# Two chained transformer blocks: experts' rows fetched by indirect DMA, sums kept in x1's place, and weight pieces loaded as two neighbouring rows per partition

## The chip, the cores and the metric

The kernel runs on one core of one Trainium2 chip. The metric is device time in microseconds (us) of one execution; the profiled execution is one of these, recorded by the hardware profiler. All times below are in us unless they are marked ns. [...]

## The reference, cut to what matters

Two blocks follow each other on 512 tokens of width 1024, all in float32. The first has attention and a short convolution, merged and projected, and then a mixture of 16 experts; the second is a chain of dense layers. The change lies around the experts:

```
hx2    = rmsnorm(x1, norm2_g) * (1 + sc2) + sh2          # 512 x 1024
aff    = softmax(hx2 @ w_router)                         # 512 x 16
gate, idx = top_k(aff.T, 64)                             # each expert picks 64 tokens
xe     = hx2[idx]                                        # 16 x 64 x 1024
ye     = (silu(xe @ w_gate) * (xe @ w_up)) @ w_down * gate
x2     = x1 + g2 * scatter_add(ye, idx)
```

Each expert has three matrices of 1024 x 1024 float32, 4 MiB each: 192 MiB of weights for 64 rows per expert.

## The kernel before, in words

The program is one long list of instructions, in the order in which the code emits them. The mixture of experts comes after the first block's output projection (x1, held in SBUF as four tiles `xr` of 128 tokens) and ahead of the second block's dense layers.

**Router.** `half_T` and `half_mm` transpose x1 by pieces of 128 columns, multiply by the router weights `wr_` and fill `aff`; `s1` holds each token's inverse norm (its last step is a power on GpSimd). `router_aff` turns `aff` so that experts lie on partitions. Eight rounds of max and match_replace on VectorE mark each expert's 64 tokens, a scan numbers them, and `post` holds, per token and expert, the slot number or 0.

**Experts, in pairs.** Eight pairs p of experts (two experts share the 128 columns of TensorE, 64 slots each). `onehot(p)` compares slot numbers with 1..64: `Gu` is the 0/1 matrix token x slot, `Gs` the same times `s1`. `gather(p, k0, n)` multiplies x1 by `Gs`, 128 columns at a time, which picks, scales and transposes the tokens' rows in one step; ScalarE applies gain and shift and writes `xe`. Then come three matmuls over the weights (`pair_gemm`: `pa_` for gate, `pu` for up, `py` for down), each in four steps of two pieces (one piece of 1 MiB per expert: 256 rows of a matrix, as two blocks of 128 rows). `hb` is the activated product, transposed on TensorE ahead of the down matmul. `put_y` scales by the gate column `gt_` (made by `gates`), and `combine` adds the pair's rows to the tokens through `GT`, the transposed 0/1 matrix (made by `slots_T`); the sums live in two tiles `acc`. The gather of pair p+1 is laid between the steps of pair p's down matmul.

**Weights.** `elist` is the list of 192 MiB in the order of use: 184 pieces of 256 x 1024 (1 MiB each), and then the last pair's down matrices, 8 MiB, by column halves (512 columns). `eload` takes the next piece of the list, a free tile of the pool that a just consumed piece came from, and issues the load on SyncE's queue (SP). Twenty pieces are loaded ahead of the first matmul; from then on a load is issued when a step of `pair_gemm` has consumed a piece, except for the piece numbers in one line:

```
if i not in (3, 15, 16, 17, 18):
    eload(etiles[i][1])
```

Those five tiles go to `GT`, `hb`, `yb`, `acc` and others. A piece is laid out as `w.rearrange("(k p) n -> p k n", p=128)`: partition p gets row p and row 128 + p of the piece, two runs of 4 KB.

**Around it.** VectorE, ScalarE, GpSimd and SP each work through their own queue in order. `pw_tile` computes a product for the second block between router and experts and writes it to HBM (`pw_d`) from ScalarE's queue; it is read back late in the second block as runs of 8 KB. `x2_half` finishes x2 as the last combine's halves come, and the second block's first weights (`W.load`) stand behind the experts' in SP's queue.

Of the kernel before, what the change touches and what calls it, by code (L numbers as in the profile page):

```python
# [18 lines left out]
NT = T // 128  # L19
# [11 lines left out]

CL = _layout(("ident", 128), ("sel", 2), ("iota", 64),
             ("cos", NT * HD), ("sin", NT * HD), ("mask", 896), ("cmask", 128))


def _constants():

    c = np.zeros((128, CL["total"]), np.float32)
    p = np.arange(128)
    c[:, CL["ident"]] = np.eye(128, dtype=np.float32)  # L40
    for i in range(2):
        c[:, CL["sel"].start + i] = (p % 32 == i)
    t = np.arange(T)
    inv = np.float32(10000.0) ** (-np.arange(16, dtype=np.float32) / np.float32(16))
# [18 lines left out]
def tile_two_blocks(ctx: ExitStack, tc: tile.TileContext, a, out):  # L63
# [311 lines left out]
    ACT.activation(sT[:, :, 0:2], p_[:, :16].rearrange("p (i k) -> p k i", i=2), AF.Silu)  # L375
    modc = cp.tile([128, 48, 2], F32, name="modc")

# [165 lines left out]
    wr_ = cp.tile([128, KT, 16], F32, name="wr_")  # L543
    SP.dma_start(out=wr_, in_=a["w_router"][0].rearrange("(k p) e -> p k e", p=128))
    wk = W.parts[0]
# [208 lines left out]
    def mod_hooks(h, dst, add, after):  # L754
# [16 lines left out]
        return hooks  # L771

    def mod_columns(c, acc_):

        p_ = bank("pb", (4,))
        for j in range(4):
            PE.matmul(p_[:, j:j + 1], acc_[:, j * 128:j * 128 + 128], onec, start=True, stop=True)
        DVE.tensor_add(modc[:, c:c + 4, 0], p_, column("b_mod", c, 4))

# [222 lines left out]
    def half(n):  # L1002
        return slice(n * 512, n * 512 + 512)

    ga2 = cp.tile([128, 8], F32, name="ga2")
    DVE.tensor_scalar(ga2, modc[:, 32:40, 0], 1.0, None, op0=OP.add)
    DVE.tensor_mul(ga2, ga2, column("norm2_g", 0, 8))
    sh2 = modc[:, 24:32, 0]
    rb = cp.tile([128, 16], F32, name="rb")

    def router_prep():
# [36 lines left out]
    def half_mm(t, n):  # L1048
# [31 lines left out]
    def eload(tags):  # L1080

        for tag in tags.split():
            i = len(etiles)
            if i < len(elist) and not (tag == "wr" and i >= len(elist) - 14):
                w, k, nc_ = elist[i]
                if tag == "X":

                    t_ = [gp.tile([128, D], F32, name="ewa", tag="g1b"),
                          cp.tile([128, CL["cmask"].start - nc0], F32, name="ewb", tag="cst2")[:, 0:D]]
                    for j in range(2):  # L1090
                        SP.dma_start(out=t_[j], in_=w[128 * j:128 * j + 128])
# [98 lines left out]

    Gu, Gs = {}, {}

    def onehot(p):

        Gu[p], Gs[p] = tmp("Gu", (NT, 128)), tmp("Gs", (NT, 128))
# [3 lines left out]
        DVE.tensor_mul(Gs[p], Gu[p], s1[:, :, None].to_broadcast([128, NT, 128]))  # L1199

    onehot(0)
    def gather(p, k0, n=4):

        p_ = bank("pg", (n, 128))
        for d in range(n):
            ds = slice((k0 + d) * 128, (k0 + d) * 128 + 128)
            for t in range(NT):
                PE.matmul(p_[:, d], xrow(t, ds), Gs[p][:, t], start=(t == 0), stop=(t == NT - 1))  # L1208
        for d in range(n):
            k = k0 + d  # L1210
# [110 lines left out]
    for p in range(8):  # L1321
# [23 lines left out]
        side = []
        if p < 7:
            gather(p + 1, 0, 2)
            side = [lambda q=q: gather(p + 1, 2 * q, 2) for q in (1, 2, 3)]
# [533 lines left out]
```

## Time and profile before

| what | value |
|---|---|
| median of 3 runs | 1700.84 us (1697.22 to 1701.57) |
| profiled execution, its own time | 1697.36 us |
| its span, first to last instruction | 1695.6 us |
| mean granted TensorE clock | 0.998 |
| TensorE matmul busy | 1657.6 us (98%) |
| VectorE, ScalarE, GpSimd busy | 917.1, 582.1, 49.5 us |
| HBM read, written | 329.94 MB, 4.19 MB |

The 98% of TensorE is an average over stages with different limits, and matmuls are pipelined, so a busy TensorE can still be one that has to wait for data a little at each step. The page's DMA and GB/s lines cut the span in 40 slices of 42.4 us and show which stage moves how much.

### The profile page before, as it was taken

What the parts mean: (1) busy time and instruction counts of PE and PEld (TensorE: products, weight loads), DVE (VectorE), ACT (ScalarE), POOL (GpSimd) and SP (SyncE); (2) the same over time, 40 slices, a digit from 0 to 9 for tenths busy, and PEclk for the clock granted to TensorE, in tenths of its full rate; (3) what the DMA queues carried; (4) which work ended last, traced back from release to release, by engine and by line L of the source; (5) the groups of instructions that cost most, each with busy time, mean ns of one, the idle gap of its engine ahead of it and who ended that gap; (6) DMA issues with size and microseconds to landing.
All of it is one profiled execution on the core that took longest, in us unless ns stands there. A gap on an engine that the chain in (4) does not pass through costs nothing.

```text
span 1695.6 us, 21458 instructions
## 1 busy us (share of the span) xinstructions
PE 1657.6 (98%) x8704; PEld 1173.6 (69%) x8704; DVE 917.1 (54%) x1687; ACT 582.1 (34%) x1118; POOL 49.5 (3%) x59
## 2 busy tenths in 40 slices
PE   8999999989999999999999999989999999999998
PEld 5987787767888874443444344358898888877886
DVE  4667776565564442212212211257889999845555
ACT  5454444455232232110111011053435442354234
POOL 2000000000000000000000000010001000000000
PEclk9999999999999999999999999999999999999999
DMA  9232323111554669999999999953323233333241
GB/s 337 88 125 75 125 75 100 58 43 52 174 180 142 246 271 344 361 399 409 409 409 409 409 409 408 403 199 109 100 75 100 75 99 97 102 100 100 100 149 50
DMA packets 162167, 335.52 MB, mean 198 GB/s; under 512 B 6959, under 2 KB 91732, under 8 KB 161812
## 3 DMA queue, kind: packets, MB, share of 16 engines
q1 hardware_dynamic: 159376, 328.50, 53.4%
q0 software_dynamic: 1168, 2.89, 0.5%
q10 hardware_dynamic: 1524, 2.76, 0.4%
q8 instruction: 68, 1.11, 0.3%
q14 instruction: 31, 0.25, 0.0%
HBM read 329.94 MB, written 4.19 MB: 197 GB/s over the span
## 4 chain that ended last, share of the span: by engine, by line
PE 90%; DVE 6%; ACT 2%; issue 1%; DMA 1%; POOL 0%; SPq 0%; POOLq 0%; ACTq 0%; DVEq 0%
PE pb L294 15%; PE pb L295 15%; PE pb L296 15%; PE pu L1244 7%; PE py L1244 6%; PE pg L1208 4%; PE po L873 2%; PE pT L865 2%; PE s L834 1%; PE pg L1265 1%; PE pv L295 1%; PE pv L296 1%; PE pv L294 1%; PE pa__5938 L1244 1%; PE pa__7273 L1244 1%
## 5 line engine op out<-in xcount | busy, mean ns | idle before, releaser
L253 DVE TENSOR_TENSOR wl<-wr,wh 128x512 fp32r<-128x512 f32 x340 | 230.1, 696 | 119.6 <-ACT wh L255 119.6
L255 ACT ACTIVATE wh<-wr 128x512 fp32r<-128x512 f32 x340 | 194.6, 620 | 104.8 <-PE pb L295 58.9
L1593 DVE SCALAR_TENSOR_TENSOR co<-cin,cols,co 128x512 f32<-128x512 f32 x240 | 191.5, 798 | 4.2
L294 PE MATMUL pb<-h2h,wh 128*128 128x512 f32 x432 | 170.8, 395 | 0.0
L296 PE MATMUL pb<-h2h,wl 128*128 128x512 f32 x432 | 168.3, 390 | 0.0
L295 PE MATMUL pb<-h2l,wh 128*128 128x512 f32 x432 | 168.2, 389 | 0.0
L294 PE MATMUL pb<-hxh,wh 128*128 128x512 f32 x320 | 130.1, 406 | 0.0
L295 PE MATMUL pb<-hxl,wh 128*128 128x512 f32 x320 | 125.3, 392 | 0.0
L296 PE MATMUL pb<-hxh,wl 128*128 128x512 f32 x320 | 125.3, 391 | 0.0
L1244 PE MATMUL pu<-ew,xe 128*64 128x512 f32 x512 | 116.0, 595 | 0.0
L1244 PE MATMUL py<-ew,hb 128*64 128x512 f32 x440 | 101.0, 597 | 0.0
L294 PEld LDWEIGHTS pb<-h2h,wh 128*128 128x128 f32 x432 | 81.1, 188 | 18.9 <-issue 2.4
L296 PEld LDWEIGHTS pb<-h2h,wl 128*128 128x128 f32 x432 | 81.1, 188 | 17.1
L295 PEld LDWEIGHTS pb<-h2l,wh 128*128 128x128 f32 x432 | 81.2, 188 | 16.9 <-issue 0.5
L1279 DVE SCALAR_TENSOR_TENSOR yt<-py,gt__5666,g2b 128x512 f32<-128x512 f32 x15 | 10.6, 747 | 143.8 <-PE py L1244 136.3
L1244 PEld LDWEIGHTS pu<-ew,xe 128*64 128x64 f32 x512 | 36.4, 137 | 66.4 <-issue 64.6
L844 ACT ACTIVATE P<-P,m 128x512 f32<-128x512 f32 (+1 forms) x64 | 49.7, 777 | 85.6 <-DVE m L843 83.1
L840 DVE CUSTOM_DVE_ANT_0 P<-s,cst,sink 128x512 f32<-128x512 f32 (+1 forms) x64 | 52.2, 816 | 46.0 <-PE s L837 45.7
L1211 ACT ACTIVATE xe<-pg,modc,ga 128x128 f32<-128x128 f32 x64 | 25.8, 453 | 147.0 <-PE pg L1208 140.5
L1208 PEld LDWEIGHTS pg<-Gs,xr 128*128 128x128 f32 x512 | 59.5, 191 | 20.9 <-issue 19.5
L296 PEld LDWEIGHTS pb<-hxh,wl 128*128 128x128 f32 x320 | 60.0, 188 | 13.3
L294 PEld LDWEIGHTS pb<-hxh,wh 128*128 128x128 f32 x320 | 60.2, 188 | 11.4 <-issue 2.3
(453 smaller groups left out, 3066.9 us busy)
## 6 DMA issues: line engine op xcount, KB each, us to landing
ew<-w_exp_gate SPq DMA_DIRECT2D x64, 1024.0 KB, 18.1
ew<-w_exp_up SPq DMA_DIRECT2D x64, 1024.0 KB, 16.7
ew<-w_exp_down SPq DMA_DIRECT2D x59, 1024.0 KB, 15.7
wr<-w_in SPq DMA_DIRECT2D x58, 1024.0 KB, 5.8
wr<-w_mod SPq DMA_DIRECT2D x16, 1024.0 KB, 5.1
wm<-w_mod SPq DMA_DIRECT2D x8, 1024.0 KB, 13.6
wr<-w_out SPq DMA_DIRECT2D x8, 1024.0 KB, 5.0
wr<-w_proj_attn SPq DMA_DIRECT2D x4, 1024.0 KB, 5.2
```

The costliest lines, as they stand in the source:

```text
L253: (lo_engine or DVE).tensor_tensor(lo[:, ks], raw[:, ks], hi[:, ks].bitcast(F32), op=OP.subtract)
L255: ACT.activation(hi[:, ks], raw[:, ks], AF.Copy)
L294: PE.matmul(ps, ah, bh, start=first, stop=False)
L295: PE.matmul(ps, ah, bl, start=False, stop=False)
L296: PE.matmul(ps, al, bh, start=False, stop=last)
L840: DVE.tensor_tensor_reduce(p_[:, :n], s2[:, self.s0:self.s0 + n], self.mask, 1.0, sink8[:, 4 * g + i:4 * g + i + 1], op0=OP.add, op1=OP.ma ...
L844: ACT.activation(p_[:, :n], p_[:, :n], AF.Exp, bias=m4[:, i:i + 1], scale=0.125, accum_out=sm[:, i:i + 1])
L865: PE.transpose(p_[:, i, :], self.P[i][:, kk * 128:kk * 128 + 128], ident)
L873: PE.matmul(po[64 * h:64 * h + 64], V[:, vi, g * 64:g * 64 + 64], last[:, :, h, :], start=(kk == 1), stop=(kk == nk), tile_position=(0, 64 ...
L1208: PE.matmul(p_[:, d], xrow(t, ds), Gs[p][:, t], start=(t == 0), stop=(t == NT - 1))
L1244: PE.matmul(ps[64 * e:64 * e + 64, n], lhs(k, e), tiles[e][kk][:, n * 512:n * 512 + 512], start=(k == 0), stop=(k == KT - 1), tile_positio ...
L1593: DVE.scalar_tensor_tensor(co[ct], cin[ct][:, k:k + 512], ctap(k, ct), co[ct], op0=OP.mult, op1=OP.add)
```

## The change

1. x1's rows are written to HBM (`x1_d`, four stores of 512 KB on ScalarE's queue) as they are finished. For pairs 1 to 7 the rows of the experts come back by an indirect DMA issued by GpSimd (128 rows of 4 KB), whose indices are made on TensorE and VectorE by `gates(p)` from the 0/1 matrix and a column of token numbers; ScalarE scales the rows by the inverse norm, `slots` transposes them on TensorE and VectorE applies gain and shift. Pair 0 is still gathered by matmul.
2. The sums go into x1's own tiles; `acc` is gone, and pieces 16 and 17 are reloaded like the others.
3. A piece is laid out as `(p k) n -> p (k n)`: partition p gets rows 2p and 2p + 1, one run of 8 KB. All that meets this order (x1's columns, `hb`, gain, shift, router weights) is read with a step of two (`dcol`). The last pair's column halves become 16 loads of 512 KB with runs of 2 KB, as before.
4. A `pad` tile and smaller `modc` move the weight tiles by 64 bytes inside a partition.

```diff
+    bmp = cp.tile([128, 32], F32, name="bmp")
+    for i, (n, o) in enumerate((("b_mod", 3072), ("b_mod", 4096), ("norm2_g", 0))):
...
+        POOL.dma_start(out=bmp[:, 8 * i:8 * i + 8].rearrange("p (q k) -> p q k", k=2), in_=v_)
...
+    def dcol(k):
+
+        return slice(256 * (k // 2) + k % 2, 256 * (k // 2) + 256, 2)
...
-            c = n * 512 + i * 128
-            PE.transpose(p_[:, i], xrow(t, slice(c, c + 128)), ident)
+            PE.transpose(p_[:, i], xrow(t, dcol(4 * n + i)), ident)
...
+            DVE.tensor_copy(aff[:, t, 17:18], s1[:, t:t + 1])
+            ACT.dma_start(out=x1_d[t * 128:t * 128 + 128], in_=xrow(t))
...
-                SP.dma_start(out=t_, in_=w.rearrange("(k p) n -> p k n", p=128))
+                for j in range(0, k, 2):
+                    SP.dma_start(out=t_[:, j:j + 2], in_=w[128 * j:128 * j + 256].rearrange("(p k) n -> p k n", k=2))
...
+        if p:
+            r = xe[:, p % 2].rearrange("p k c -> p (k c)")
+            POOL.indirect_dma_start(out=r, out_offset=None, in_=x1_d,
+                                    in_offset=bass.IndirectOffsetOnAxis(ap=ix[:, p:p + 1], axis=0))
+            ACT.activation(r, r, AF.Copy, scale=sl[:, p:p + 1])
+
+    def slots(p, n):
+
+        r = xe[:, p % 2].rearrange("p k c -> p (k c)")
+        p_ = bank("pg", (4, 128))
+        for i in range(4):
+            PE.transpose(p_[:, i], r[:, dcol(4 * n + i)], ident)
+        for i in range(4):
+            k = 4 * n + i
+            DVE.tensor_scalar(xe[:, p % 2, k], p_[:, i], ga2[:, k:k + 1], sh2[:, k:k + 1], op0=OP.mult, op1=OP.add)
...
-                if i not in (3, 15, 16, 17, 18):
+                if i not in (3, 15, 18):
...
-        DVE.tensor_add(arow(t, half(n)), p_, (arow if p else xrow)(t, half(n)))
+        DVE.tensor_add(xrow(t, half(n)), p_, xrow(t, half(n)))
...
-        side = [lambda: None, lambda: None, lambda: gates(p)] + ([lambda: slots_T(p)] if p else [])
+        side = [lambda: gates(p + 1) if p < 7 else None, lambda: gates(0) if not p else None]
...
+        if p < 6:
+            onehot(p + 2)
+        side = []
+        if p < 7:
+            slots(p + 1, 0)
+            side = [lambda: None, lambda: slots(p + 1, 1)]
```

How TensorE's queue changes, from the up matmul of pair 2 to the start of its down matmul (`pu` and `py` are the two sums, `Gs` and `xr` the matmul gather, `Gu` the 0/1 matrix). Before:

```order
L1244 MATMUL pu<-ew,xe 64x512 x16
L1218 MATMUL pg<-aff,Gu 128x2 x4
L1244 MATMUL pu<-ew,xe 64x512 x8
L1230 MATMUL pg<-cst,Gu 128x128 x4
L1244 MATMUL pu<-ew,xe 64x512 x8
L1208 MATMUL pg<-Gs,xr_5042 128x128 x2
L1208 MATMUL pg<-Gs,xr_5043 128x128 x2
L1208 MATMUL pg<-Gs,xr_5042 128x128 x2
L1208 MATMUL pg<-Gs,xr_5043 128x128 x2
L1353 MATMUL pg<-cst,hb 128x128 x8
```

And now, at the same place:

```order
L1243 MATMUL pg<-aff,Gu 128x18 x4
L1287 MATMUL pu<-ew,xe 64x512 x32
L1273 MATMUL pg<-cst,Gu 128x128 x4
L1384 MATMUL pg<-cst,hb 128x128 x8
L1261 MATMUL pg<-cst,xe 128x128 x4
L1287 MATMUL py<-ew,hb 64x512 x8
L1261 MATMUL pg<-cst,xe 128x128 x4
```

The gather's matmuls are gone; `gates` for the next pair stands ahead of the whole up matmul, and eight transposes of the fetched rows stand around the first step of the down matmul.

ScalarE's queue over one pair (`hb` the activation of the gate sums, `GT` the transposed 0/1 matrix, `yb` the pair's output). Before:

```order
L1337 ACTIVATE hb<-pa__6206 128x512 x2
L1231 ACTIVATE GT<-pg 128x512
L1211 ACTIVATE xe<-pg,modc,ga_5046 128x128 x2
L1358 ACTIVATE hb<-pg 128x512
L1211 ACTIVATE xe<-pg,modc,ga_5046 128x128 x6
L1280 ACTIVATE yb<-yt 128x512 x2
```

And now, at the same place:

```order
L1374 ACTIVATE hb<-pa__6187 128x512 x2
L1254 ACTIVATE xe<-xe,sl 128x1024
L1274 ACTIVATE GT<-pg 128x512
L1389 ACTIVATE hb<-pg 128x512
L1317 ACTIVATE yb<-yt 128x512 x2
```

One pass over the fetched rows, which waits for the indirect DMA, has come ahead of `GT` and of the copy of `hb` that the down matmul needs.

## Rows read from the trace of the kernel before

**Rows 1.** The page: GB/s in 40 slices, and all DMA packets by size.
```profile
GB/s 337 88 125 75 125 75 100 58 43 52 174 180 142 246 271 344 361 399 409 409 409 409 409 409 408 403 199 109 100 75 100 75 99 97 102 100 100 100 149 50
DMA packets 162167, 335.52 MB, mean 198 GB/s; under 512 B 6959, under 2 KB 91732, under 8 KB 161812
```

**Rows 2.** Windows of the experts' stage: busy by engine, then clock, DMA share, GB/s.
```profile
668.00:686.00 18.00, 18.00 (x88) 6.48 (x86) 1.69 (x4) 1.08 (x2) 0.00 (x0) 1.00 0.93 365
686.00:700.00 14.00, 13.54 (x82) 7.35 (x79) 1.98 (x3) 2.69 (x6) 0.00 (x0) 1.00 0.90 358
700.00:720.00 20.00, 20.00 (x104) 9.11 (x103) 4.30 (x7) 2.87 (x6) 0.00 (x0) 1.00 0.92 343
720.00:740.00 20.00, 19.69 (x91) 7.42 (x92) 5.32 (x10) 1.08 (x2) 0.00 (x0) 1.00 1.01 388
760.00:1060.00 300.00, 296.12 (x1506) 130.47 (x1506) 57.73 (x95) 33.93 (x72) 0.00 (x0) 1.00 1.03 409
1100.00:1112.00 12.00, 11.44 (x48) 3.46 (x48) 2.60 (x8) 0.63 (x1) 0.00 (x0) 1.00 1.05 386
```

**Rows 3.** Timeline of SP's queue: start, duration, what; pair 1's gate pieces.
```profile
668.80 14.77 SPq L1096 DMA_DIRECT2D ew<-w_exp_gate  x8
```

**Rows 4.** Chain of waits near the stage's end: start, duration, what.
```profile
1098.51 11.78 DMA ew<-w_exp_down
```

**Rows 5.** Timeline of TensorE: pair 2's and 3's first steps; last expert matmuls.
```profile
769.15 3.60 PE L1244 MATMUL pa__6206<-ew,xe 128*64 128x512 f32 x16
...
827.58 2.74 PE L1244 MATMUL pa__6472<-ew,xe 128*64 128x512 f32 x12
...
1116.31 1.94 PE L1400 MATMUL py<-ew,hb 128*64 128x512 f32 x8
```

**Rows 6.** Groups by form in pair 2: busy, mean ns, idle before.
```profile
L1208 PE MATMUL pg<-Gs,xr 128*128 128x128 f32 x64 | 8.2, 281 | 0.0
L1208 PEld LDWEIGHTS pg<-Gs,xr 128*128 128x128 f32 x64 | 7.4, 191 | 2.5 <-issue 2.4
L1353 PE MATMUL pg<-cst,hb 128*128 128x128 f32 x8 | 1.3, 279 | 0.5 <-ACT xe L1211 0.5
```

**Rows 7.** DMA answer, 1634 to 1641: read-back of pw_d in 8 KB runs.
```profile
DMA packets 576, 2.59 MB, mean 371 GB/s; under 512 B 32, under 2 KB 32, under 8 KB 335
```

**Rows 8.** Windows in that read-back, columns as in rows 2.
```profile
1634.00:1635.00 1.00, 1.00 (x6) 0.84 (x5) 1.00 (x3) 0.00 (x0) 0.00 (x0) 1.00 1.07 416
1635.00:1636.00 1.00, 1.00 (x6) 0.84 (x5) 1.00 (x3) 0.00 (x0) 0.00 (x0) 1.00 1.12 451
1636.00:1637.00 1.00, 1.00 (x6) 0.81 (x6) 0.62 (x2) 0.28 (x1) 0.00 (x0) 1.00 1.04 442
```

**Rows 9.** DMA answer, 981 to 989: a 512 KB load on ScalarE's queue.
```profile
q10 hardware_dynamic: 144, 0.52, 16.5%
...
ew<-w_exp_gate SPq DMA_DIRECT2D x4, 1024.0 KB, 18.7
```

**Rows 10.** The tile fng, loaded there: its issue.
```profile
L1362 ACTq DMA_DIRECT2D fng<-final_norm_g x1: 339/339/339, 981.9 to 981.9; - x1
```

**Rows 11.** Line, timeline and group rows nearest to the new small steps.
```profile
L1221 DVE COPY gt__5666<-pg x16: 149/156/163, 679.6 to 1088.7; 64x1 f32<-64x1 f32 x16
...
1500.02 0.53 POOL L169 DMA_DIRECT2D g2bfinal_g<-final_g  x1 [0.81 <-PE pvar L1609]
...
L417 ACT ACTIVATE x<-x,rs 128x1024 f32<-128x1024 f32 x2 | 2.3, 1149 | 2.0 <-POOL rs L179 2.0
```

**Rows 12.** Chain of waits at the router's last token tile.
```profile
630.20 0.55 POOL s L179
630.78 0.25 DVE lg L1057
```

**Rows 13.** Windows after the last expert matmul, columns as in rows 2.
```profile
1122.00:1125.00 3.00, 1.11 (x3) 0.19 (x1) 2.90 (x9) 2.84 (x9) 0.70 (x1) 1.00 0.00 0
1125.00:1128.60 3.60, 2.79 (x13) 2.82 (x14) 3.15 (x15) 2.75 (x8) 1.70 (x3) 0.53 0.00 0
```

More of the change, by code (lines that the diff above doesn't have):

```diff
@@ L29, in _layout @@
     return out
-CL = _layout(("ident", 128), ("sel", 2), ("iota", 64),
+CL = _layout(("ident", 128), ("sel", 2), ("tok", NT), ("iota", 64),
              ("cos", NT * HD), ("sin", NT * HD), ("mask", 896), ("cmask", 128))
@@ L43, in _constants @@
     t = np.arange(T)
+    c[:, CL["tok"]] = t.reshape(NT, 128).T
     inv = np.float32(10000.0) ** (-np.arange(16, dtype=np.float32) / np.float32(16))
@@ L170, in brows @@
         return t_
+    cp.tile([128, 16], F32, name="pad")
     mhalf = cp.tile([128, 1], F32, name="mhalf")
@@ L375, in tile_two_blocks @@
     ACT.activation(sT[:, :, 0:2], p_[:, :16].rearrange("p (i k) -> p k i", i=2), AF.Silu)
-    modc = cp.tile([128, 48, 2], F32, name="modc")
+    modc = cp.tile([128, 16, 2], F32, name="modc")
+    modd = cp.tile([128, 16], F32, name="modd")
     def put_cols(gi, n=128):
@@ L543, in tile_two_blocks @@
     wr_ = cp.tile([128, KT, 16], F32, name="wr_")
-    SP.dma_start(out=wr_, in_=a["w_router"][0].rearrange("(k p) e -> p k e", p=128))
+    SP.dma_start(out=wr_.rearrange("p (q k) e -> p q (k e)", k=2), in_=a["w_router"][0].rearrange("(q p k) e -> p q (k e)", p=128, k=2))
     wk = W.parts[0]
@@ L776, in mod_columns @@
         for j in range(4):
-            PE.matmul(p_[:, j:j + 1], acc_[:, j * 128:j * 128 + 128], onec, start=True, stop=True)
-        DVE.tensor_add(modc[:, c:c + 4, 0], p_, column("b_mod", c, 4))
+            cs = slice(256 * (j // 2) + j % 2, 256 * (j // 2) + 256, 2)
+            PE.matmul(p_[:, j:j + 1], acc_[:, cs], onec, start=True, stop=True)
+        DVE.tensor_add(modd[:, c - 24:c - 20], p_, bmp[:, c - 24:c - 20])
     def conv_posts(j):
@@ L1003, in half @@
         return slice(n * 512, n * 512 + 512)
+    def dcol(k):
+        return slice(256 * (k // 2) + k % 2, 256 * (k // 2) + 256, 2)
     ga2 = cp.tile([128, 8], F32, name="ga2")
-    DVE.tensor_scalar(ga2, modc[:, 32:40, 0], 1.0, None, op0=OP.add)
-    DVE.tensor_mul(ga2, ga2, column("norm2_g", 0, 8))
-    sh2 = modc[:, 24:32, 0]
+    DVE.tensor_scalar(ga2, modd[:, 8:16], 1.0, None, op0=OP.add)
+    DVE.tensor_mul(ga2, ga2, bmp[:, 16:24])
+    sh2 = modd[:, 0:8]
     rb = cp.tile([128, 16], F32, name="rb")
@@ L1020, in tile_two_blocks @@
     DVE.memset(aff, 0.0)
+    DVE.tensor_copy(aff[:, :, 16], C("tok"))
+    x1_d = dp.tile([T, D], F32, name="x1_d")
     s1 = cp.tile([128, 4], F32, name="s1")
@@ L1090, in eload @@
                     for j in range(2):
-                        SP.dma_start(out=t_[j], in_=w[128 * j:128 * j + 128])
+                        SP.dma_start(out=t_[j], in_=w.rearrange("(p k) n -> p k n", k=2)[:, j])
                     etiles.append((t_, tag))
@@ L1189, in tile_two_blocks @@
     warm2(4)
-    Gu, Gs = {}, {}
+    Gu = {}
     def onehot(p):
-        Gu[p], Gs[p] = tmp("Gu", (NT, 128)), tmp("Gs", (NT, 128))
+        Gu[p] = tmp("Gu", (NT, 128))
         DVE.tensor_tensor(Gu[p].rearrange("p t (e s) -> p t e s", e=2),
@@ L1198, in onehot, with gather @@
                           post[:, :, 2 * p:2 * p + 2, None].to_broadcast([128, NT, 2, 64]), op=OP.is_equal)
-        DVE.tensor_mul(Gs[p], Gu[p], s1[:, :, None].to_broadcast([128, NT, 128]))
     onehot(0)
-    def gather(p, k0, n=4):
+    Gs = tmp("Gs", (NT, 128))
+    DVE.tensor_mul(Gs, Gu[0], s1[:, :, None].to_broadcast([128, NT, 128]))
+    onehot(1)
+    def gather(k0, n):
         p_ = bank("pg", (n, 128))
         for d in range(n):
-            ds = slice((k0 + d) * 128, (k0 + d) * 128 + 128)
@@ L1207, in gather @@
             for t in range(NT):
-                PE.matmul(p_[:, d], xrow(t, ds), Gs[p][:, t], start=(t == 0), stop=(t == NT - 1))
+                PE.matmul(p_[:, d], xrow(t, dcol(k0 + d)), Gs[:, t], start=(t == 0), stop=(t == NT - 1))
         for d in range(n):
             k = k0 + d
-            ACT.activation(xe[:, p % 2, k], p_[:, d], AF.Identity, bias=sh2[:, k:k + 1], scale=ga2[:, k:k + 1])
+            ACT.activation(xe[:, 0, k], p_[:, d], AF.Identity, bias=sh2[:, k:k + 1], scale=ga2[:, k:k + 1])
@@ L1213, in tile_two_blocks @@
     gt_ = cp.tile([128, 8], F32, name="gt_")
+    sl = cp.tile([128, 8], F32, name="sl")
+    ix = cp.tile([128, 8], mybir.dt.uint32, name="ix")
     def gates(p):
-        p_ = bank("pg", (2,))
+        p_ = bank("pg", (18,))
         for t in range(NT):
-            PE.matmul(p_, Gu[p][:, t], aff[:, t, 2 * p:2 * p + 2], start=(t == 0), stop=(t == NT - 1))
+            PE.matmul(p_, Gu[p][:, t], aff[:, t, 0:18], start=(t == 0), stop=(t == NT - 1))
+        if p:
+            DVE.tensor_copy(ix[:, p:p + 1], p_[:, 16:17])
+            DVE.tensor_copy(sl[:, p:p + 1], p_[:, 17:18])
@@ L1219, in gates @@
         for e in range(2):
             es = slice(64 * e, 64 * e + 64)
-            DVE.tensor_copy(gt_[es, p:p + 1], p_[es, e:e + 1])
+            DVE.tensor_copy(gt_[es, p:p + 1], p_[es, 2 * p + e:2 * p + e + 1])
+        if p:
+            r = xe[:, p % 2].rearrange("p k c -> p (k c)")
+            POOL.indirect_dma_start(out=r, out_offset=None, in_=x1_d,
+                                    in_offset=bass.IndirectOffsetOnAxis(ap=ix[:, p:p + 1], axis=0))
+            ACT.activation(r, r, AF.Copy, scale=sl[:, p:p + 1])
@@ L1246, in pair_gemm @@
             for i in range(i0 + 2 * q, i0 + 2 * q + 2):
-                if i not in (3, 15, 16, 17, 18):
+                if i not in (3, 15, 18):
                     eload(etiles[i][1])
     ybuf = {}
-    acc = []
-    def arow(t, s=slice(None)):
-        return acc[t // 2][:, t % 2, s]
     def combine_half(p, t, n):
-        if not acc:
-            acc.extend(big(f"acc{i}", [2, D]) for i in range(2))
         p_ = bank("pg")
@@ L1295, in x2_half @@
         combine_half(7, t, n)
-        DVE.tensor_mul(xrow2(t, half(n)), arow(t, half(n)), fng[:, half(n)])
-        for i, row in enumerate((arow, xrow2)):
+        DVE.tensor_mul(xrow2(t, half(n)), xrow(t, half(n)), fng[:, half(n)])
+        for i, row in enumerate((xrow, xrow2)):
             ACT.activation(tile_("sqx"), row(t, half(n)), AF.Square, scale=D ** -0.5,
@@ L1329, in tile_two_blocks @@
         if p == 0:
-            gather(0, 0, 2)
-            side = [lambda q=q: gather(0, 2 * q, 2) for q in (1, 2, 3)]
+            gather(0, 2)
+            side = [lambda q=q: gather(2 * q, 2) for q in (1, 2, 3)]
         else:
@@ L1338, in tile_two_blocks @@
         pu = bank3("pu")
-        side = [lambda: None, lambda: None, lambda: gates(p)] + ([lambda: slots_T(p)] if p else [])
+        side = [lambda: gates(p + 1) if p < 7 else None, lambda: gates(0) if not p else None]
         pair_gemm(pu, i0 + 8, xlhs, side)
-        if p < 7:
-            onehot(p + 1)
         for n in range(2):
             DVE.tensor_mul(hb[:, 0, n * 512:n * 512 + 512], pu[:, n], hb[:, 0, n * 512:n * 512 + 512])
[L1345 to L1348, printed above, removed]
+        slots_T(p)
         for n in range(2):
@@ L1351, in tile_two_blocks @@
             for i in range(4):
-                c = n * 512 + i * 128
-                PE.transpose(p_[:, i], hb[:, 0, c:c + 128], ident)
+                PE.transpose(p_[:, i], hb[:, 0, dcol(4 * n + i)], ident)
             d_ = hb[:, 1, n * 512:n * 512 + 512].rearrange("p (a b) -> p a b", b=128)
@@ L1362, in tile_two_blocks @@
             ACT.dma_start(out=fng, in_=brow("final_norm_g", 0, D))
-        if p == 0:
-            side.insert(0, lambda: slots_T(0))
         py = bank3("py")
```

1 line of the change is left out of this document (added).

## The prediction

> **What bounds the kernel now.** I read the page's slices first: GB/s lies near 100 for most of the span, climbs to 399 and stays at 409 for nearly seven slices [rows 1]. That is the experts' stage. Its windows come next: from 760 to 1060 TensorE is busy 296.1 of 300 us and the DMA share is 1.03 at 409 GB/s [rows 2]. Both look full, so the question is which one ends last. TensorE's timeline gives a period of 827.58 - 769.15 = 58.43 us per pair [rows 5]. One pair's weights are 24 pieces of 1,048,576 bytes, 25.17e6 bytes, and need 61.5 us at 409 GB/s. TensorE is therefore the faster of the two by 3 us per pair and lives on pieces loaded ahead. Near the end the stock is used up: the chain of waits goes through a down-weight transfer for 11.78 us [rows 4]. TensorE and DMA are nearly in balance over the stage; taking work from TensorE alone gives little.
>
> **How long the weights take.** Pair 1's first load is issued at 668.80 [rows 3]; pieces 24 to 191 are left then: 160 MiB (167.8e6 bytes) in 4 KB runs and 8 MiB (8.39e6) in 2 KB runs. From there to 740 the rate is under 409: the deficits of the four windows are 44 x 18 + 51 x 14 + 66 x 20 + 21 x 20 = 3,246 GB/s x us, or 7.9 us [rows 2]. They are the time in which too few tiles were free. The sum is 668.8 + 167.8e6/409 (410.2) + 8.39e6/386 (21.7) + `fng` 0.52e6/409 (1.3) + 7.9 = 1109.9. The last four-matmul group of the last matmul starts at 1116.31 [rows 5]; the 6.4 us left are pieces under way at 668.80, instruction loads and the last landing, and I keep them as they are.
>
> **The change, part by part.** *TensorE.* Seven of eight gathers go. In pair 2 one costs 8.2 us of matmul time; eight transposes of the fetched rows, priced by the eight of `hb` at 1.3 us, replace it [rows 6]. The gather also covered VectorE's product `hb` after the up matmul; I charge 1 us of waiting there. A pair falls to 58.4 - 8.2 + 1.3 + 1.0 = 52.5 us. `gates` at 18 columns in place of 2 moves few columns and I cost it at nothing, hidden by the weights. So TensorE is no longer the end: seven pairs save about 41 us there, and the weights are what is late next.
>
> *Buffers.* Two more tiles go round (pieces 16 and 17 are reloaded), and pair 0's down matmul has no gather between its steps. A step of 16 matmul records frees two pieces in 3.6 us [rows 5], against 2 x 2.5 us of transfer. I take the 7.9 us as gone.
>
> *Rate.* This decides. Fetch time per run follows from the two rates: a 2 KB run takes 2048 x 16/386 = 84.9 ns on one of 16 engines, a 4 KB run 4096 x 16/409 = 160.2 ns [rows 2]. The second 2 KB cost 75.3 ns, so 9.6 ns are fixed per run, and 8 KB would take 9.6 + 301.4 = 311 ns: 421 GB/s. Are 8 KB runs carried as one? The read-back of `pw_d` has them: of 576 packets 335 are under 8 KB, 241 are not [rows 7], and its three full windows give 416, 451 and 442, mean 436 [rows 8]. Slices of 1 us with packets put into the slice they start in are rough, so I take 421 and keep 409 (no gain) and 436 as ends. The shift by 64 bytes has no row: every expert tile lies the same way before. Its effect is inside the same two ends, and I take none.
>
> [...]
>
> *Added traffic.* Seven gathers of 512 KB are 3.67e6 bytes, 9.0 us at 409, and on the path, since the DMA is full. Storing x1 (2.1e6 bytes) falls into slices at 246 to 344 GB/s [rows 1]; the room up to 409 in the slice at 271 alone is 138 x 42.4 = 5.9e6 bytes, so it costs nothing. The three small `bmp` loads stand on GpSimd's queue early, when DMA moves 88 GB/s and GpSimd has nothing else until the router.
>
> *Sum for the weights.* 668.8 + 167.8e6/421 (398.6) + 21.7 + 1.3 + 9.0 + 6.4 = 1105.8 against 1116.3: 10.5 us earlier. At 409 it is 1117.4 (1.1 later), at 436 1092.1 (24.2 earlier). Check against TensorE: one pair now brings 25.17e6/421 + 1.3 = 61.1 us of transfer against 52.5 of matmuls, so the DMA sets the end in all three.
>
> *Router.* VectorE's copy of `s1` into `aff` waits for GpSimd's power, 0.55 us, and is put ahead of `lg`, which took 0.25 us right behind it [rows 12]. At most 0.8, at least one small copy of 0.15 [rows 11]; I take 0.5. ScalarE's four store issues stand where it waits for VectorE. What follows the experts is unchanged and moves along.
>
> *The fetched rows.* New is a wait on ScalarE: its scaling pass stands ahead of `GT` and of the `hb` copy. The path is `gates` (eight records at the gather's 8.2/64, 1.0) [rows 6], four VectorE copies of 0.156, GpSimd's issue 0.53, transfer, scaling 1.15 [rows 11]. For the transfer the nearest row is `fng`, 512 KB on another queue than the weights: issued at 981.9, all 0.52 MB inside the window that ends at 989, so at most 7.1, while weights waited 18.7 to land [rows 9, 10]. Sum 10.4 us, against four up steps of 5.0 us each at the new rate. Cover: about 20 us, so I cost it at nothing.
>
> Total: -10.5 + 0.5 = -10.0, from the profiled execution's 1697.36: **1687 us**. The median of the runs shown is 3.5 above that execution and their spread 4.4, so I leave the figure and let the range carry it. A measurement of this kernel can tell about 0.3%, 5 us, from no change.
>
> **Rivals.** *The rate stays at 409.* For it: the extrapolation rests on two rates, and nothing shows a long stream of 8 KB runs. Against: rows 7 and 8. Time 1697.4 + 1.1 + 0.5 = 1699, no change.
>
> *The gathers land late* (the slower side). GpSimd's own queue never shows beside a full DMA before, and indirect addressing not at all. Pairs lose nothing until the path passes the 20 us of cover plus the 8.6 us by which TensorE is ahead of the DMA per pair: the point is about 29 us, three times my sum. In line with the weights (18.7) it would be 22, still hidden. At 45 us each pair loses 16, and seven make 112: about 1799.
>
> [...]
>
> *Reading every second column costs TensorE.* No row shows a stride of two. If it doubled weight loads of 0.191 us [rows 6], the 64 of pair 0's gather cost 12.2 and 32 router transposes at most 6.1; three quarters of the first delay the restart of the loads: 9 + 6 = 15, to 1702. Later transposes lie under the weights.
>
> *The clock.* TensorE will wait some 1.5 us in each 5 us step. It fell to 0.53 after a stretch with 1.11 busy of 3.00 [rows 13], which is emptier than 3.5 of 5. If it fell and stayed, a pair's steps would double (+42) and pass the DMA by 33: eight pairs make 264, about 1950.
>
> **How the numbers follow.** Forecast (rates from 417 to 436) 0.64, all of it faster. A rate that stays at 409, or under 417, 0.16 and, of the stride rival's 0.07, 0.04: no change, 0.20. Late gathers 0.09, clock 0.03, the rest of the stride and what I do not see 0.04: slower, 0.16. The forecast's own range is 1673 to 1691. The range takes in the rate that stays and the stride rival: 1672 to 1702; late gathers and clock are left out.
>
> **What would show it.** Right: near 23,900 packets of 8 KB or more (184 pieces of 128, and the 355 there are now [rows 1]); windows of the experts' stage near 421; a period near 61 us per pair; TensorE busy near 86% there (52.5 of 61.1), with waits for weight transfers before the steps; the group of the matmul gather, L1208 now, cut to an eighth; the last expert matmul near 1106. Wrong: 409 in those windows; ScalarE's scaling pass named as what the `hb` copies or TensorE wait for; clock under 1.00 inside the stage; pair 0 starting late.

## The result, and the profile after

The changed kernel takes **1683.64 us** (median of 4 runs, 1681.97 to 1684.48) against 1699.19 us of the kernel before on the same chip (median of 4, 1697.22 to 1701.57): ratio 0.9909, 95% interval 0.9893 to 0.9926. The forecast was 1687, range 1672 to 1702. The profiled execution took 1681.97 us, 15.4 less than the profiled one of before, where 10.0 were forecast.

The page of the changed kernel, its GB/s and its packets, answers to [rows 1]:

```profile
GB/s 366 63 110 91 102 99 101 51 51 51 151 187 139 214 299 352 423 426 426 426 426 427 427 426 427 419 209 88 88 86 91 91 85 101 101 99 101 100 151 50
DMA packets 139972, 341.26 MB, mean 203 GB/s; under 512 B 6783, under 2 KB 91556, under 8 KB 116196
```

139,972 - 116,196 = 23,776 packets have 8 KB or more, near the 23,900 forecast. An 8 KB run does travel as one, and the plateau, eight slices at 426 or 427, lies above the 421 of the forecast. The windows of the same stretches as [rows 2] (length, then busy time of TensorE, its weight loads, VectorE, ScalarE and GpSimd, then clock, DMA share, GB/s):

```profile
668.00:686.00 18.00, 18.00 (x92) 7.06 (x90) 0.76 (x6) 3.19 (x4) 1.08 (x1) 1.00 0.86 349
686.00:700.00 14.00, 13.68 (x68) 5.76 (x66) 5.22 (x12) 1.19 (x2) 0.00 (x0) 1.00 1.01 426
700.00:720.00 20.00, 20.00 (x92) 6.91 (x88) 5.28 (x8) 1.23 (x2) 0.00 (x0) 1.00 1.01 426
720.00:740.00 20.00, 19.69 (x94) 7.49 (x92) 3.02 (x8) 2.24 (x3) 0.95 (x1) 1.00 1.01 426
760.00:1040.00 280.00, 261.29 (x1164) 106.35 (x1160) 66.74 (x139) 23.31 (x35) 4.69 (x5) 1.00 1.01 426
1060.00:1085.00 25.00, 21.43 (x91) 7.64 (x90) 3.25 (x6) 1.23 (x3) 0.00 (x0) 1.00 1.02 420
1092.00:1098.00 6.00, 6.00 (x25) 1.81 (x22) 1.44 (x2) 0.63 (x1) 0.00 (x0) 1.00 1.05 407
```

The gaps of 686 to 740 are filled; the one of 668 to 686 stays. The last row, 2 KB runs, stands at 407 where before it was 386, although the change leaves those runs 2 KB long. TensorE is busy 21.43 of 25 us near the end. That is the 86% forecast for the stage, but it holds only there: over 760 to 1040 it is 261.29 of 280 us, 93%. The clock is 1.00 in all these windows. What TensorE waited for from 655 to 1100 (total us, times, longest):

```profile
PE pu L1287 <- DMA ew<-w_exp_up: 12.9, 9, 2.0
PE py L1287 <- DMA ew<-w_exp_down: 4.0, 4, 1.4
```

Three waits of 1.3 us for gate weights come on top, and waits of at most 0.3 us for VectorE. ScalarE's scaling pass and the fetched rows are not in this list. The chain of waits shows the same: before, it ran through one transfer near the end [rows 4], now from 1029 to 1084 through nothing else, and then through the matmuls:

```profile
1029.11 19.42 DMA ew<-w_exp_gate
1048.59 19.62 DMA ew<-w_exp_up
1068.29 16.03 DMA ew<-w_exp_down
...
1086.50 11.41 PE py L1435 x48
```

TensorE's timeline, the starts of pairs 2 and 3 and the last expert matmuls, answers to [rows 5]; between them the gate matmuls of pairs 5 and 6 (count, ns, first and last start):

```profile
759.35 3.60 PE L1287 MATMUL pa__6187<-ew,xe 128*64 128x512 f32 x16
...
811.23 3.60 PE L1287 MATMUL pa__6429<-ew,xe 128*64 128x512 f32 x16
...
L1287 PE MATMUL pa__6913<-ew,xe x64: 592/592/643, 922.4 to 943.9; 128*64 128x512 f32 x64
...
L1287 PE MATMUL pa__7158<-ew,xe x64: 592/592/643, 983.8 to 1005.2; 128*64 128x512 f32 x64
...
1101.95 1.94 PE L1435 MATMUL py<-ew,hb 128*64 128x512 f32 x8
```

A pair that TensorE does not have to wait in takes 51.9 us (52.5 forecast, 58.4 before). Pairs 0 to 3 go at that pace (51.9 to 52.1 us), on pieces loaded ahead; the period of 61 us that was forecast for the stage comes only with pairs 4 to 6 (983.8 - 922.4 = 61.4 for pair 5). The last group starts at 1101.95 instead of 1116.31: of the 15.4 us, 14.4 are won by the end of the experts. The remaining 1 us is not the change's: before, the clock stood at 0.53 for 3.6 us right behind the experts [rows 13], and in this execution it did not. In kernel d1 below, whose code at that place is the changed kernel's, it is 0.57 from 1115.2 to 1119.2 us.

### The profile page after: what moved, and what is told of

The parts are those of the page before. It is cut to its first block, busy times and chain, and to the rows that moved or that the text cites. A ratio compares the mean times of both kernels' runs of the same rounds, so it can differ in the third digit from the quotient of the medians.

```text
span 1680.1 us, 20745 instructions
## 1 busy us (share of the span) xinstructions
PE 1623.8 (97%) x8312; PEld 1145.9 (68%) x8312; DVE 931.4 (55%) x1755; ACT 569.0 (34%) x1069; POOL 58.7 (3%) x69
## 2 busy tenths in 40 slices
DMA packets 139972, 341.26 MB, mean 203 GB/s; under 512 B 6783, under 2 KB 91556, under 8 KB 116196
## 4 chain that ended last, share of the span: by engine, by line
PE 75%; DMA 15%; DVE 6%; issue 2%; ACT 2%; POOL 0%; SPq 0%; POOLq 0%; ACTq 0%; DVEq 0%
PE pb L297 15%; PE pb L298 15%; PE pb L299 15%; DMA ew<-w_exp_gate 5%; DMA ew<-w_exp_down 5%; DMA ew<-w_exp_up 5%; PE py L1287 3%; PE po L884 2%; PE pu L1287 2%; PE pT L876 2%; PE s L845 1%; PE pv L298 1%; PE pv L297 1%; PE pv L299 1%; PE pa__6429 L1287 1%
## 5 line engine op out<-in xcount | busy, mean ns | idle before, releaser
L1379 DVE TENSOR_TENSOR hb<-pu,hb 128x512 f32<-128x512 f32 x16 | 10.3, 686 | 126.2 <-PE pu L1287 63.1
L1304 DVE TENSOR_TENSOR xr<-pg,xr 128x512 f32<-128x512 f32 x64 | 41.6, 687 | 68.8 <-PE pg L1303 67.6
L1287 PEld LDWEIGHTS py<-ew,hb 128*64 128x64 f32 x440 | 32.6, 137 | 61.4 <-issue 49.7
L299 PEld LDWEIGHTS pb<-hxh,wl 128*128 128x128 f32 x320 | 60.1, 188 | 13.5
```

Source lines behind the costliest of these rows:

```text
L299: PE.matmul(ps, al, bh, start=False, stop=last)
L1287: PE.matmul(ps[64 * e:64 * e + 64, n], lhs(k, e), tiles[e][kk][:, n * 512:n * 512 + 512], start=(k == 0), stop=(k == KT - 1), tile_positio ...
L1304: DVE.tensor_add(xrow(t, half(n)), p_, xrow(t, half(n)))
```

## The experiments

Ten kernels, each timed against the kernel before. Three questions: what made the stream faster, whether one half of the change would do, and how much room the fetched rows have. First the rate.

**a1: tiles back in their old place, 8 KB runs kept.**

```diff
-    cp.tile([128, 16], F32, name="pad")
```

> The changed kernel without the pad tile, so that every weight tile begins 64 bytes further on, modulo 128, as before the change; runs stay 8 KB. Theory 'both': a run carries a fixed time, and the place of the tile changes it. The 2 KB runs went at 386 GB/s before and at 405 after, 84.9 and 80.9 ns each, and the 1 KB runs of the first 20 us at 349 and 386, 46.9 and 42.4 ns: about 4.3 ns less per run at either size. An 8 KB run then takes 308 + 4 = 312 ns here: 420 GB/s in the experts' windows, the 2 KB runs of 1090 to 1100 back near 386, and the first 20 us back near 349. 171.5e6 bytes at 420 instead of 426 are 5.7 us more, 8.4e6 in 2 KB runs 1.0 more: about 1690 us, ratio 0.995. Rival 'length alone': 426 stays, 1684 us. Rival 'place alone': 409 in the windows, 16.7 us more, about 1700 us, no gain over the kernel before.

Measured: 1690.47 us, ratio 0.9950 (0.9937 to 0.9963). Windows, columns as above; 10 to 20 us is the start of the kernel, where 1 KB runs are loaded:

```profile
10.00:20.00 10.00, 9.77 (x64) 5.17 (x62) 4.08 (x11) 4.06 (x9) 0.71 (x1) 1.00 1.09 348
760.00:1040.00 280.00, 259.92 (x1144) 104.41 (x1142) 66.34 (x137) 23.30 (x35) 4.69 (x5) 0.99 1.01 421
1092.00:1098.00 6.00, 5.71 (x30) 2.81 (x30) 2.21 (x8) 1.20 (x2) 0.00 (x0) 1.00 1.05 386
```

421, 386 and 348 against 426, 407 and 386: with the tiles 64 bytes lower all three sizes of run lose. At the old place the extrapolation from run lengths alone, 421, is exact.

**a2: 4 KB runs as before, tiles in the new place** (the router's rows, bias columns and transposes follow the old order).

```diff
-                for j in range(0, k, 2):
-                    SP.dma_start(out=t_[:, j:j + 2], in_=w[128 * j:128 * j + 256].rearrange("(p k) n -> p k n", k=2))
+                SP.dma_start(out=t_, in_=w.rearrange("(k p) n -> p k n", p=128))
...
-        return slice(256 * (k // 2) + k % 2, 256 * (k // 2) + 256, 2)
+        return slice(128 * k, 128 * k + 128)
```

> The changed kernel with the pieces laid out as before (one 4 KB row per partition and run, contiguous columns instead of every second one), the tiles still where the change puts them. Theory 'both': a 4 KB run took 160.2 ns at 409 GB/s and takes 4.3 less: 155.9 ns, 420 GB/s in the experts' windows; about 5.7 us more than the changed kernel, 1689 us, ratio 0.995. Rival 'length alone': 409, 16.7 us more, about 1700 us. Rival 'place alone': 426, 1683 us. Pair 0's gather loses its stride: 32 matmuls in 3.8 us instead of 4.0.

Measured: 1687.36 us, ratio 0.9939 (0.9926 to 0.9951).

```profile
760.00:1040.00 280.00, 257.34 (x1137) 101.25 (x1134) 64.39 (x135) 22.05 (x33) 4.69 (x5) 1.00 1.03 419
```

419: a 4 KB run takes 4096 x 16 / 419 = 156.4 ns instead of 160.2. Both rivals (409 and 426) are out; place and length each count.

**a3: both undone.** What is left are the gathers by indirect DMA, the sums in x1's place and two more tiles that go round (the edits of a1 and a2 together).

> The changed kernel with both undone: 4 KB runs, tiles 64 bytes further on. What is left of the change are the gathers by indirect DMA, the sums in x1's place and the two more tiles that go round. All theories of the rate: 409 GB/s in the windows. If DMA sets the end, the 3.67e6 bytes of the gathers cost what the two tiles bring: about 1700 us, ratio 1.000, although TensorE has 6 us less to do per pair. Rival (TensorE's work set the end before): faster than the kernel before by 10 us or more, ratio 0.994 or less.

Measured: 1701.07 us, ratio 1.0013 (1.0005 to 1.0022): no gain.

```profile
760.00:1040.00 280.00, 252.21 (x1093) 91.31 (x1092) 60.96 (x126) 21.80 (x33) 4.69 (x5) 1.00 1.03 409
...
1118.15 1.94 PE L1433 MATMUL py<-ew,hb 128*64 128x512 f32 x8
```

The rate is 409 again, TensorE waits 16.8 us for up weights and 9.2 for down weights, and the last group starts at 1118.15. A pair without waits takes TensorE 51.6 us instead of 58.4, and the stream holds the end where it was. Two things cancel in the stream: the gathers' 3.67e6 bytes cost 9.0 us at 409, and the gaps of 686 to 740 are gone (407 to 410 there, against 343 to 388 before [rows 2]).

**f1: tiles 128 bytes lower** (the pad tile out, one small tile narrowed, two of one column merged).

```diff
-    cp.tile([128, 16], F32, name="pad")
...
-    bmp = cp.tile([128, 32], F32, name="bmp")
+    bmp = cp.tile([128, 24], F32, name="bmp")
...
```

> The changed kernel with every weight tile begun 128 bytes lower: at 128 modulo 256 instead of 0. In the kernel with 8 KB runs alone the tiles lie at 128 modulo 256 too, and its first 20 us ran at 349 GB/s like a misaligned one. Theory '256': only a tile that begins at a multiple of 256 bytes saves the 4.3 ns per run: first 20 us near 349 GB/s, experts' windows 420 to 421, 2 KB runs of 1090 to 1100 near 387, about 1690 us, ratio 0.995. Rival '128': a multiple of 128 is enough: 386, 426, 406 and 1684 us, ratio 0.991; the slow start of the other kernel then has another cause.

Measured: 1686.96 us, ratio 0.9928 (0.9915 to 0.9940), between the two.

```profile
10.00:20.00 10.00, 10.00 (x65) 5.28 (x64) 4.90 (x12) 4.91 (x9) 0.70 (x1) 1.00 1.10 348
760.00:1040.00 280.00, 263.17 (x1158) 105.46 (x1156) 67.09 (x139) 23.29 (x35) 4.68 (x5) 0.99 1.01 424
1092.00:1098.00 6.00, 6.00 (x30) 2.41 (x27) 0.77 (x2) 0.63 (x1) 0.00 (x0) 1.00 1.05 399
```

1 KB runs lose all of it (348), 2 KB and 8 KB runs about 40% (399 and 424). But "a multiple of 256" is not the answer either. In the programs as built the expert tiles do not all lie alike: of the last 160 loads of 1 MiB, 103 begin at a multiple of 256 and 57 at 128 modulo 256 in the changed kernel, and in f1 it is the other way round. The packet records of the traces, put to 135 loads of the middle in their order, show no loss for the changed kernel's group at 128: its packets of 8 KB take 309.3 ns in the mean, the others 309.5. In f1, 38% of the packets of the group at 128 take more than 310 ns, and 6% of the others. So f1's smaller loss at 8 KB is in part that of a mixture, and which starts cost time, and why, stays open; shown is only what moving all tiles by 64 or 128 bytes does.

Next, whether one half would do.

**b1: 8 KB runs alone.** The kernel before, with its gathers by matmul, in the new layout.

```diff
-                SP.dma_start(out=t_, in_=w.rearrange("(k p) n -> p k n", p=128))
+                for j in range(0, k, 2):
+                    SP.dma_start(out=t_[:, j:j + 2], in_=w[128 * j:128 * j + 256].rearrange("(p k) n -> p k n", k=2))
...
-            ds = slice((k0 + d) * 128, (k0 + d) * 128 + 128)
+            ds = dcol(k0 + d)
```

> The kernel before with 8 KB runs and aligned tiles alone: TensorE still gathers every pair's rows by matmuls, no row goes by indirect DMA, five tiles are not reloaded. Theory 'nearly in balance': the faster stream only uncovers TensorE, whose pairs take 58.4 us whatever the weights do: period 58 to 59 us for every pair, last expert matmul near 1113 to 1116, 1694 to 1698 us, ratio 0.997 to 0.999; DMA in the windows at 25.17e6 / 58.4 = 431 at most, so 426 with short gaps. Rival 'DMA alone sets the end': 8.6 us of gather traffic less than the changed kernel at the same rate, last expert matmul near 1091, 1675 us, ratio 0.986.

Measured: 1700.37 us, ratio 1.0010 (1.0002 to 1.0019). No gain, and 2 us above the forecast: a pair takes 58.8 us, 0.4 more than before, with a gather that reads every second column. Its tiles lay where f1 has them, not where the changed kernel has them, as its start at 348 GB/s gave away; that led to f1 and to the next kernel.

**b2: the same with the tiles at the changed kernel's place** (a pad of 128 bytes more).

> The kernel before with 8 KB runs and the tiles at multiples of 256 bytes, as the changed kernel has them: TensorE still gathers every pair's rows by matmuls. In the kernel with 8 KB runs alone the tiles lay at 128 modulo 256, which cost a part of the rate (424 instead of 426); that excuse is gone here. Theory 'TensorE holds it': period 58.8 us per pair as there (58.4, and 0.4 for reading every second column in the gather), no wait of TensorE for a weight transfer, last four-matmul group of the experts at 1114 to 1117, 1698 to 1701 us, ratio 0.999 to 1.001; the first 20 us at 386 GB/s. Rival 'the last GB/s were missing': 1690 us or less, ratio 0.995 or less.

Measured: 1700.40 us, ratio 1.0008 (0.9999 to 1.0017). Windows, then TensorE's timeline:

```profile
700.00:720.00 20.00, 20.00 (x106) 9.10 (x104) 4.05 (x6) 2.88 (x6) 0.00 (x0) 1.00 0.77 287
760.00:1040.00 280.00, 276.70 (x1378) 120.61 (x1376) 55.73 (x92) 30.96 (x65) 0.00 (x0) 1.00 1.01 425
```

```profile
772.34 3.17 PE L1256 MATMUL pa__6212<-ew,xe 128*64 128x512 f32 x14
...
831.14 3.17 PE L1256 MATMUL pa__6478<-ew,xe 128*64 128x512 f32 x14
...
1118.26 1.94 PE L1411 MATMUL py<-ew,hb 128*64 128x512 f32 x8
```

The stream has its 425, stands still at the start instead (287 from 700 to 720; for lack of free tiles, as I read it), and TensorE, which waits for no weights, needs 58.8 us per pair. The last group starts at 1118.26, behind the 1114 to 1117 expected; pair 0 had begun 2.1 us later than in the kernel before. This is the mirror image of a3: either half alone is worth nothing, the two together 15 us.

Last, the fetched rows and the buffers.

**d1: the old list of tiles that do not go round again.**

```diff
-                if i not in (3, 15, 18):
+                if i not in (3, 15, 16, 17, 18):
```

> The changed kernel with the old list of tiles that do not go round again (pieces 3, 15, 16, 17, 18 instead of 3, 15, 18): two tiles of 1 MiB less in flight from pair 0's down matmul on. Theory (my prediction's 7.9 us of gaps came from too few tiles): the DMA stands still for up to 2 x 2.46 = 4.9 us once, near 700 to 720, and the stream ends that much later: up to 1688.5 us. Rival: TensorE frees tiles every 52 us per 24, 484 GB/s, faster than the DMA fills them, so the two tiles bring nothing after the first pairs: 1684 us, windows of 686 to 740 at 426.

Measured: 1686.20 us, ratio 0.9925 (0.9912 to 0.9938). The window of 700 to 720:

```profile
700.00:720.00 20.00, 20.00 (x92) 7.05 (x90) 5.33 (x8) 1.26 (x2) 0.00 (x0) 1.00 0.93 386
```

40 x 20 / 426 = 1.9 us of stream are lost there. The median is 2.6 us later, and so is the last group, counted from pair 1's first load (433.7 us against 431.1): the two tiles are worth about half of the upper bound.

**d2: the gather issued three steps later.**

```diff
-        side = [lambda: gates(p + 1) if p < 7 else None, lambda: gates(0) if not p else None]
+        side = [lambda: None, lambda: gates(0) if not p else None, lambda: None, lambda: gates(p + 1) if p < 7 else None]
```

> The changed kernel with the gates of the next pair, and so its indirect gather, put before the fourth step of the up matmul instead of the first: some 13 us later in the first pairs, 15 in the later ones. The gather's path was 12 to 13 us in the trace (1.0 matmuls, 0.6 copies, 0.5 issue, about 9 in transfer, 1.2 scaling), and only one step of 5 us is left ahead of the transposes. Theory 'slack': TensorE waits 7 to 9 us per pair, about what it is ahead of the DMA (60.3 - 51.9 = 8.4 us per pair), so the end moves little: 1684 to 1690 us, with ScalarE's scaling pass as what TensorE waits for. Rival 'on the path': seven pairs lose 7 us each and the experts end 49 us later: 1733 us, ratio 1.02.

Measured: 1708.78 us, ratio 1.0052 (1.0039 to 1.0066): slower than before the change, and halfway between theory and rival. TensorE's stop in pair 0, and the windows around it:

```profile
699.46 1.13 PE L1384 MATMUL pg<-cst,hb 128*128 128x128 f32 x4 [6.01 <-ACT GT L1274]
```

```profile
693.40:696.40 3.00, 0.05 (x1) 0.00 (x0) 0.00 (x0) 0.00 (x0) 0.00 (x0) 1.00 1.00 419
696.40:699.40 3.00, 0.00 (x0) 0.00 (x0) 0.00 (x0) 1.62 (x3) 0.00 (x0) 0.58 0.99 416
699.40:703.20 3.80, 3.74 (x14) 2.17 (x16) 2.57 (x6) 0.50 (x2) 0.00 (x0) 0.50 0.82 345
```

TensorE stops for 6 us behind ScalarE, whose `GT` copy is queued behind the scaling pass, and then works 3.7 us at a clock of 0.50. A pair takes 60.1 us (first steps of pairs 0 and 7 at 657.38 and 1078.05, 420.67 / 7), 8.2 more than 51.9. My slack "per pair" was the mistake. The account that I made afterwards: the 16 pieces that lie ready when pair 0 begins let the stream end long before eight times 60.3. TensorE alone would be through at 655.4 + 8 x 51.9 = 1070.6, the stream lets it end at about 1103, so some 33 us may be lost over all pairs. Seven stops of 8.2 are 57, 24 too many; measured are 25.

**d4: the gather issued two steps later**, to test that account (the same edit, with `gates(p + 1)` third).

> The changed kernel with the gates of the next pair, and so its gather, put before the third step of the up matmul: 7.2 us later in pairs 1 to 3, 10 in the later ones. The path from the gates to the scaled rows is 12.05 us in the changed kernel's trace (673.75 to 685.80), and from the gates to the transposes of the fetched rows 18.4 us in pair 0, 17.3 in the next: TensorE stops about 2 us per pair. Theory 'one account for all pairs': TensorE could end its eight pairs at 655.4 + 8 x 51.9 = 1070.6, and the stream lets it end near 1103; 33 us may be lost over all pairs before the end moves. The kernel with the gates before the fourth step lost 7 x 8.2 = 57 us, 24 too many, and was 25 us later. Here 7 x 2 = 14 us or less are lost: 1684 to 1686 us, ratio 0.991 to 0.992, clock 1.00. Rival 'every stop is paid': 14 us more, 1698 us, ratio 0.999.

Measured: 1687.79 us, ratio 0.9931 (0.9917 to 0.9944). The account is nearer than the rival, and 2 to 4 us off. TensorE waited 15.8 us behind ScalarE in all, a little over the 14 of the forecast. Against the forecast the clock fell behind five of the six stops of 2.3 to 3.1 us, and the stream stood still a little for want of free tiles (373 against 426 from 700 to 720 are 53 x 20 / 426 = 2.5 us):

```profile
698.00:702.00 4.00, 4.00 (x16) 1.13 (x12) 1.22 (x4) 0.00 (x0) 0.00 (x0) 0.73 1.02 426
...
700.00:720.00 20.00, 20.00 (x94) 7.01 (x92) 5.36 (x10) 1.23 (x2) 0.00 (x0) 1.00 0.94 373
```

A stop in the first pairs is thus not wholly free: it also holds back the tiles that the stream waits for.

**d3: the gathers of pairs 2 to 7 left out**, so that these pairs compute on other rows.

```diff
-            POOL.indirect_dma_start(out=r, out_offset=None, in_=x1_d,
-                                    in_offset=bass.IndirectOffsetOnAxis(ap=ix[:, p:p + 1], axis=0))
+            if p == 1:
+                POOL.indirect_dma_start(out=r, out_offset=None, in_=x1_d,
+                                        in_offset=bass.IndirectOffsetOnAxis(ap=ix[:, p:p + 1], axis=0))
```

> The changed kernel with the indirect gathers of pairs 2 to 7 left out (pair 1's stays), so those pairs compute on rows that were not fetched: 3.15e6 bytes less. Theory (the DMA sets the end, and a gather costs its bytes): 3.15e6 / 426 = 7.4 us less, 1676 us, ratio 0.987; windows stay at 426, period 59.1 instead of 60.3 us. Rival 'dearer than their bytes' (packets on GpSimd's queue disturb the others): 10 us or more less, windows above 426. Rival 'they fall into gaps': 1684 us, no change.

Measured: 1676.72 us, ratio 0.9864 (0.9848 to 0.9881).

```profile
760.00:1040.00 280.00, 265.87 (x1190) 104.70 (x1186) 67.48 (x140) 23.29 (x35) 0.00 (x0) 1.00 1.01 427
```

Six gathers cost 6.9 us where their bytes are 7.4 us of stream: within the noise they cost their bytes, and the rate beside them is the same.

## Why the prediction was right, step by step

**What bounds the kernel.** "Nearly in balance; taking work from TensorE alone gives little" holds in both directions: b2 speeds the stream and leaves TensorE as it was (ratio 1.0008), a3 frees TensorE and leaves the rate as it was (1.0013). a3 is not TensorE alone, since it also adds the gathers' bytes and closes gaps; at 409 these two cancel. The sum went by the weights, and TensorE's 51.9 us per pair against 25.17e6 / 426 + 1.2 = 60.3 of transfer left the stream as the end. What the prediction did not see is when: TensorE runs out of pieces loaded ahead only in pair 4, so a period near 61 us holds for the second half of the stage and not for all of it.

**Rate.** The step that was mis-sized is "The shift by 64 bytes has no row: [...] and I take none". The two rates of [rows 2] did give what length brings: 421 at the old place (a1). The place brings the rest. Time per run is size x 16 / rate:

```
run     changed kernel's place  64 bytes lower          loss
1 KB    386 GB/s   42.4 ns      348 GB/s   47.1 ns      4.6 ns
2 KB    407        80.5         386        84.9         4.4
4 KB    419       156.4         409       160.2         3.8
8 KB    426       307.7         421       311.3         3.7
```

With 37.8 ns taken off per KB, an estimate from (307.7 - 156.4) / 4, a run carries about 5 ns at the new place and 9 at the old, at each of the four lengths. Longer runs have fewer of these to carry, so the two edits do not simply add: place alone brings 10 GB/s, length alone 12, both 17.

**The sum**, term by term. The stream's start was forecast at 668.8 and came at 670.8:

```profile
670.84 15.93 SPq L1116 DMA_DIRECT2D ew<-w_exp_gate  x8
```

4 KB pieces, now 8 KB runs: 398.6 forecast, 167.8e6 / 426 = 393.9. Runs of 2 KB: 21.7, now 8.39e6 / 407 = 20.6. Gathers: 9.0, now 3.67e6 / 426 = 8.6. The buffer gaps, 7.9 us and "taken as gone", are 77 x 18 / 426 = 3.3 us in one window; d1 shows that the two more tiles closed 2 of what went. The rest went with the other half, TensorE's shorter pairs: b2, without it, still stands at 287 from 700 to 720. With 1.2 for `fng` this makes 1098.4, and 3.5 us are left to the end at 1101.95 where I kept 6.4. So 3.9 us came on top of the 10.5. That is a balance of errors of both signs, and in part luck: the rates and the end were 9 us better than in the sum, the start and the gap 5 us worse. Why the end needs 3 us less is not shown.

**Router.** 0.5 forecast. The copy stands between the power and `lg`, as said:

```profile
632.21 0.15 DVE L1064 COPY aff<-s 128x1 f32<-128x1 f32 x1 [0.66 <-POOL s L182]
632.27 0.16 DVE L1075 TENSOR_TENSOR lg<-lg,pl 128x16 f32<-128x16 f32 x1
```

From the last token tile's `s` to the top-k it is 634.69 - 631.20 = 3.49 us, against 633.00 - 629.77 = 3.23. Pair 0 began at 655.40 instead of 653.53; most of that was lost ahead of the router. A part changes from one execution to the next (below), but perhaps not all: pair 0 begins between 654.98 and 657.38 in all nine traces with 8 KB runs and at 653.5 to 653.6 in the three with 4 KB runs. No run settles what the layout costs there.

**The fetched rows**, pair 1: gates, GpSimd's issue, ScalarE's scaling, the transposes that use them:

```profile
673.75 1.07 PE L1243 MATMUL pg<-aff,Gu 128*128 128x18 f32 x8
...
675.83 1.08 POOL L1252 DMA_INDIRECT xe<-x_d,ix  x1 [43.66 <-DVE gt__5684 L1249]
...
684.65 1.15 ACT L1254 ACTIVATE xe<-xe,sl 128x1024 f32<-128x1024 f32 x1 [9.67 <-issue]
...
692.16 0.74 PE L1261 MATMUL pg<-cst,xe 128*128 128x128 f32 x4
```

The path is 685.80 - 673.75 = 12.05 us where 10.4 was forecast, its cover 18.4 where I took 20: hidden, as said. Two terms were too small: GpSimd's issue took 0.94 to 1.08 us where I had 0.53, and the rows landed in 8.2 to 9.6 where I had at most 7.1. What was wrong in the rival is its point. The "8.6 us by which TensorE is ahead per pair" do not add up over the pairs; by d2 the allowance is about 33 us in all, and by d4 stops that stay below it are not free (4 us for 15.8). By these two I estimate that late gathers would have begun to cost past the cover of 17.3 us and cost nearly in full from about 22 (17.3 and 33 / 7), not from 29.

**The other rivals.** Every second column: in pair 2 of b2 a weight load of the gather takes 196 ns and the group 8.5 us, against 191 and 8.2 [rows 6]; nothing doubles. The clock: 1.00 through the changed kernel's stage, where TensorE's longest single wait for weights was 2.0 us; behind longer stops it fell in d2 and d4: to 0.50 behind one of 6.01 us (699.4 to 703.2, d2), to 0.73 behind one of 2.57 us (698 to 702, d4).

## What to carry to other kernels

When two resources are full in the same stage, price each half of a change alone: here neither half brought anything, because the other resource, or the bytes that the half added, held the end. Ask of every DMA stream both how long its runs are and where the tile begins: one pad of 64 bytes was worth 7 us here, two fifths of the gain. And count slack over the whole stage, with what is loaded ahead, not pair by pair.

## What the runs showed that I had not expected

The start of the kernel told of the tiles' place before any expert ran: 1 KB runs went at 384 to 386 GB/s in every kernel with the tiles at the changed kernel's place and at 348 in the others, the kernel before among them. It was the cheapest place to see it.

Behind a TensorE stop of 6 us the clock was 0.50 through the 3.7 us of work that followed (d2); stops of 2.3 to 3.1 us were followed by a lower clock in five of six cases (d4: 0.73 from 698 to 702 and 0.65 from 752 to 756 behind the first two).

The clock also dips where no kernel differs. d3 is the changed kernel up to pair 1, yet in its execution the clock was 0.83 in 28 to 38 us, where the changed kernel's was 1.00, and pair 0 began at 657.34 instead of 655.40:

```profile
28.00:38.00 10.00, 9.95 (x62) 8.37 (x62) 6.33 (x14) 5.23 (x8) 4.36 (x7) 0.83 1.09 385
```

Two profiled executions of this kernel can thus differ by 2 us for no reason in their code, which is why the terms above are read from rates and periods and not from single start times.
